# Weight gradient on one core: the second slice of X is loaded by the software DMA queue as bf16 instead of by a hardware queue as f32

## The chip, the cores and the metric

The kernel runs on one NeuronCore of one Trainium2 chip. The metric is the device time of one execution in microseconds (us). Profiles are of one execution each; they show the span from the first to the last instruction, which is somewhat shorter than the device time of the same execution.

Engines: TensorE (PE; PEld is its weight load), VectorE (DVE), ScalarE (ACT), GpSimd (POOL) and SyncE (SP). A DMA that SP or ACT issues runs on a hardware queue (q1 and q10 in this trace); one that POOL issues runs on the software queue (q0)[...].

## The reference

```
# input: [16, 512, 1024] f32, grad_output: [16, 512, 768] f32
grad_weight = np.einsum('bmk,bmn->kn', input, grad_output)   # [1024, 768] f32
```

With batch and m taken together this is X^T G with X of 8192 x 1024 and G of 8192 x 768: a sum over 8192 rows.

## The kernel before

**Slices and units.** The 8192 rows are cut into 64 slices of 128 rows (P = 128). A slice of X is 128 x 1024 and one of G 128 x 768. Two slices make a unit; there are 32 units, u = 0 to 31. A letter in LOADS (line 12) says how a unit is multiplied. For "s" (units 0 to 6, 30 and 31) each slice is multiplied on its own: X has a left and a right half of 512 columns, G of 384, and the four products of halves are the sums A (left, left), B (left, right), C (right, left) and D (right, right). For "P" (units 7 to 29) the two slices are treated as a 2 x 2 arrangement of blocks and multiplied with seven products (A, D, m, n, o, p, q) in place of eight; DVE first makes the sums and differences of blocks that these need (functions sum_g1 to sum_x3, lines 125 to 154).

**Matmuls.** Each product of halves takes four matmuls (q = 0 to 3, one for every 128 columns of the half of X) of 128 x 128 by 128 x 384 in bf16 (line 285), each into a PSUM bank of its own. Two slots of four banks are in use in turn. When a step closes, its banks are added to or copied into f32 sums in SBUF, by DVE (lines 301 and 303) or by ACT (line 299); before some steps ACT first puts the old sum into the bank (line 266).

**Order.** The engines' programs are written by hand. ORDER (lines 16 to 28) is a list of steps. "D1:1" means that product D is taken up to item 1 (an item is a slice of an "s" unit, or a "P" unit), and that ACT evicts one of its banks; "!" closes the step and evicts its banks. The first steps are A1, D1, C2, B2, D3, A2, B4, A3, C4, A4, D5, D6. A1 and D1 need slice 0 alone. C2 takes, for each q, first slice 0 and then slice 1, so its second matmul is the first to use slice 1. D3 begins the use of slice 2, B4 that of slice 3, D5 that of unit 2, B7 and B8 that of unit 3.

**Loads.** All of X and G comes from HBM as f32. From unit 2 on (u >= MERGED = 2), POOL issues one DMA for G and one for X of a whole unit (lines 106 and 107), which are rounded to bf16 on their way. Units 0 and 1 are loaded slice by slice, also by POOL (lines 111 and 113). Exceptions are G of slice 0 and X of slices 0 and 1. They are loaded as f32 into the tiles gf and xf[0], xf[1] by hardware queues: gf in two halves by SP (lines 81 and 83), xf[0] and xf[1] by ACT (lines 82 and 84). DVE and ACT then round them to bf16 (function round_by, line 206). X of slice 1 is rounded in four pieces ahead of step C2 (lines 361 to 366), the right half of gf ahead of D1 (line 360). POOL holds at most eight of its DMAs in flight: each issue waits until the eighth before it has landed. Tiles for X and G of unit 1 and later come from pools of 14 buffers each (PAIRS_HELD); xf[0], xf[1] and gf take their first buffers from the same pools.

**Start.** While the first operands are on their way, TensorE runs 12 warming matmuls on constants (lines 88 to 95).

Of the kernel before, what the change touches and what calls it, by code (L numbers as in the profile page):

```python
# [9 lines left out]
P = 128  # L10
# [28 lines left out]
MERGED = 2  # L39
# [3 lines left out]
def kernel(  # L43
# [6 lines left out]
    nc = tc.nc  # L50
    bf16 = mybir.dt.bfloat16
    f32 = mybir.dt.float32

    B, M, K = input.shape
# [6 lines left out]
    X = input.rearrange("b m k -> (b m) k")  # L61
# [4 lines left out]
    pairs = ctx.enter_context(tc.tile_pool(name="pairs", bufs=PAIRS_HELD))  # L66
# [9 lines left out]
    E = mybir.EngineType  # L76
    ctx.enter_context(tc.manual_schedule(engines={E.PE, E.DVE, E.Activation, E.Pool}))

    xf = [pairs.tile([P, K], f32, name=f"xf{s}", tag="xp") for s in range(2)]
    gf = pairs.tile([P, N], f32, name="gf", tag="gp")  # L80
    nc.sync.dma_start(out=gf[:, 0:NH], in_=G[0:P, 0:NH])  # L81
    nc.scalar.dma_start(out=xf[0], in_=X[0:P, :])
    nc.sync.dma_start(out=gf[:, NH:N], in_=G[0:P, NH:N])
    nc.scalar.dma_start(out=xf[1], in_=X[P : 2 * P, :])

    ones = nc.const_aps.tensor(1.0, (P, P), bf16)
    wps = psum.tile([P, 512], f32, name="bank7")
# [10 lines left out]
    items = []  # L98
    xg = []
    for u, kind in enumerate(LOADS):  # L100
        pool = pairs if u else head
        xp = pool.tile([P, 2, K], bf16, name="xp", tag="xp")
        gp = pool.tile([P, 2, N], bf16, name="gp", tag="gp")
        if u >= MERGED:
            rows = slice(2 * u * P, 2 * (u + 1) * P)
            nc.gpsimd.dma_start(out=gp, in_=G[rows, :].rearrange("(p m) n -> p m n", m=2))  # L106
            nc.gpsimd.dma_start(out=xp, in_=X[rows, :].rearrange("(p m) k -> p m k", m=2))  # L107
        for h in range(2):
            s = 2 * u + h
            if s > 0 and u < MERGED:  # L110
                nc.gpsimd.dma_start(out=gp[:, h, :], in_=G[s * P : (s + 1) * P, :])
            if s > 1 and u < MERGED:
                nc.gpsimd.dma_start(out=xp[:, h, :], in_=X[s * P : (s + 1) * P, :])
            if kind == "s":
                items.append(("s", xp[:, h, :], gp[:, h, :]))
        if kind == "P":
            items.append(("P", xp, gp))
        xg.append((xp, gp))
# [79 lines left out]
    def fill(n):  # L198
        for _ in range(n):
            f, i = filler.pop()  # L200
            f(i)


    def round_by(engine, dst, src, c0, c1):
        copy = nc.vector.tensor_copy if engine == "DVE" else nc.scalar.copy
        copy(out=dst[:, c0:c1], in_=src[:, c0:c1])  # L206

    x0, x1, g0 = items[0][1], items[1][1], items[0][2]
    round_by("DVE", g0, gf, 0, 192)
    round_by("ACT", g0, gf, 192, NH)  # L210
    round_by("DVE", x0, xf[0], 0, P)
# [35 lines left out]
    done = {p: 0 for p in streams}  # L247
# [101 lines left out]
            del opened[p]  # L349
            slots.append(slot)  # L350

    rounded = False
    for n, step in enumerate(ORDER):
        step, _, ahead = step.partition("!")
        step, _, byact = step.partition(":")
        byact, first = byact[:1], byact[1:]
        at = next(c for c in step if c.isalpha())
        before, upto = step.split(at)
        if n == 1:
            round_by("DVE", g0, gf, NH, N)  # L360
        if not rounded and done[at] < 2 <= int(upto):
            rounded = True
            round_by("DVE", x1, xf[1], 4 * P, 6 * P)
            round_by("ACT", x1, xf[1], 6 * P, 8 * P)
            round_by("DVE", x1, xf[1], 0, 2 * P)
            round_by("ACT", x1, xf[1], 2 * P, 4 * P)
        fill(int(before or 0))
        ahead = [int(a) for a in ahead.split(",")] if ahead else None
        visit(at, int(upto), int(byact or 0), first, ahead is not None, ahead, n == len(ORDER) - 1)
# [31 lines left out]
```

## Time and profile before

| | |
|---|---|
| device time, median of 3 runs | 163.57 us (163.35 to 163.69) |
| profiled execution | 163.7 us, span 161.9 us |
| PE busy | 157.1 us (97%), 951 matmuls |
| DVE busy | 139.6 us (86%) |
| ACT busy | 94.6 us (58%) |
| POOL busy | 34.6 us (21%) |
| HBM | 58.72 MB read, 3.15 MB written, 382 GB/s over the span |
| DMA by queue | software 28.64 MB (as written, bf16), hardware 3.47 and 1.11 MB |

The profile's groups of instructions give the operations around the change. xf is rounded by DVE in 222 to 295 ns a piece (128 or 256 columns) and by ACT in 401 to 405 ns (256 columns). The hardware DMAs of xf land 4.1 and 5.9 us after their issue, those of gf 3.8 and 5.5 us after it. POOL takes some 0.53 to 0.6 us for the issue of one DMA. The granted TensorE clock is full throughout.

How to read it: the busy share of an engine says little of what sets the time. The chain of work that ended last does: it is followed back from the last instruction, at each step to what released it. The page's sum of this chain is PE 93%, DMA 3%, DVE 1%. The timeline lists instructions in order of time, with the idle time before each in brackets and what ended it.

### The profile page before, as it was taken

The page shows a single profiled execution, that of the slowest core. Times are in us where ns is not written, and L with a number is a line of the kernel's source. Part 1 is how long each engine was busy: PE and PEld are TensorE (multiplying, and loading weights), DVE is VectorE, ACT ScalarE, POOL GpSimd, SP SyncE. Part 2 cuts the span into 40 slices and gives each one's busy share as a digit, 9 for nine tenths or more (in the row PEclk, how much of TensorE's full clock was granted, in tenths as well). Part 3 has the DMA queues.
Part 4 walks back from the last instruction along what each step waited for, and adds up shares of the span by engine and source line. Part 5 has one row for each costly group of instructions (what it writes and reads, how often), then busy time and mean ns, then how long its engine had stood idle before and what let it go on. Part 6 is the DMA issues. An engine that isn't in the chain of part 4 may idle for free.

```text
span 161.9 us, 2755 instructions
## 1 busy us (share of the span) xinstructions
PE 157.1 (97%) x951; PEld 92.7 (57%) x951; DVE 139.6 (86%) x289; ACT 94.6 (58%) x221; POOL 34.6 (21%) x69
## 2 busy tenths in 40 slices
PE   8799999999999999999999999999999999999992
PEld 2365666566565565655656666666555666666661
DVE  0557947469979999999989999999998999999992
ACT  3766004745587799359749684661446646888410
POOL 7442222122221212222212222222212100000000
PEclk9999999999999999999999999999999999999999
DMA  5999999999999999999999999999999999902675
GB/s 171 294 213 211 211 216 215 211 211 215 214 213 212 212 213 213 213 211 215 212 213 213 212 216 214 220 207 212 211 211 214 212 214 214 187 5 97 225 283 173
DMA packets 12397, 33.40 MB, mean 206 GB/s; under 512 B 1376, under 2 KB 4192, under 8 KB 12384
## 3 DMA queue, kind: packets, MB, share of 16 engines
q0 software_dynamic: 9360, 28.64, 89.4%
q1 hardware_dynamic: 2592, 3.47, 6.2%
q10 hardware_dynamic: 432, 1.11, 1.8%
q8 instruction: 7, 0.11, 0.3%
q14 instruction: 6, 0.05, 0.1%
HBM read 58.72 MB, written 3.15 MB: 382 GB/s over the span
## 4 chain that ended last, share of the span: by engine, by line
PE 93%; DMA 3%; DVE 1%; SPq 0%; issue 0%
PE bank L285 93%; DMA gf<-in_grad_output_dram 3%; PE bank L336 0%; DVE acc L344 0%; SPq L81 0%; DVE gp L206 0%
## 5 line engine op out<-in xcount | busy, mean ns | idle before, releaser
L285 PEld LDWEIGHTS <-xp 128*128 128x128 bf16 x649 | 63.3, 98 | 43.6 <-issue 1.5
L285 PE MATMUL bank<-gp,xp 128*128 128x384 bf16 x468 | 80.9, 326 | 1.0 <-DVE gp L206 1.0
L299 ACT COPY macc<-bank 128x384 f32<-128x384 f32 x73 | 31.5, 493 | 25.0 <-PE bank L285 24.9
L303 DVE TENSOR_TENSOR acc<-bank,acc 128x384 f32<-128x384 f32 x69 | 34.7, 551 | 8.7 <-PE bank L285 8.3
L285 PEld LDWEIGHTS <-xe 128*128 128x128 bf16 x276 | 26.6, 98 | 18.5 <-DVE xe L145 0.8
L285 PE MATMUL bank<-ge,xp 128*128 128x384 bf16 x181 | 33.6, 326 | 0.0
L285 PE MATMUL bank<-gp,xe 128*128 128x384 bf16 x184 | 32.4, 326 | 0.0
L266 ACT COPY bank<-macc 128x384 f32<-128x384 f32 x56 | 25.3, 503 | 8.0 <-DVE macc L303 6.9
L299 ACT COPY acc<-bank 128x384 f32<-128x384 f32 x44 | 19.5, 486 | 15.4 <-PE bank L285 15.3
L107 POOL DMA_DIRECT2D xp<-in_input_dram x30 | 15.9, 530 | 53.1 <-DMA xp<-in_input_dram 29.8
L106 POOL DMA_DIRECT2D gp<-in_grad_output_dram x30 | 15.9, 531 | 37.5 <-DMA gp<-in_grad_output_dram 14.8
L303 DVE TENSOR_TENSOR macc<-bank,macc 128x384 f32<-128x384 f32 x44 | 22.5, 552 | 1.5 <-PE bank L285 1.2
L266 ACT COPY bank<-acc 128x384 f32<-128x384 f32 x34 | 15.2, 492 | 8.6 <-DVE acc L303 8.5
L285 PE MATMUL bank<-ge,xe 128*128 128x384 bf16 x92 | 16.6, 326 | 0.0
L145 DVE TENSOR_TENSOR xe<-xp 128x1024 bf16<-128x1024 bf16 x23 | 15.7, 684 | 0.5 <-DMA xp<-in_input_dram 0.5
L154 DVE TENSOR_TENSOR xp<-xp 128x1024 bf16<-128x1024 bf16 x23 | 15.7, 684 | 0.0
L189 DVE TENSOR_TENSOR acc<-acc,macc 128x768 f32<-128x768 f32 (+1 forms) x20 | 14.6, 791 | 0.0
L131 DVE TENSOR_TENSOR ge<-gp 128x768 bf16<-128x768 bf16 x23 | 12.7, 551 | 0.2 <-DMA gp<-in_grad_output_dram 0.2
L140 DVE TENSOR_TENSOR gp<-gp 128x768 bf16<-128x768 bf16 x23 | 12.7, 551 | 0.0
L149 DVE TENSOR_TENSOR xe<-xp 128x512 bf16<-128x512 bf16 x23 | 9.6, 418 | 0.0
L135 DVE TENSOR_TENSOR ge<-gp 128x384 bf16<-128x384 bf16 x23 | 8.1, 351 | 0.0
L89 PE MATMUL bank<-const-bfloat16-1.0 128*128 128x512 bf16 (+1 forms) x12 | 4.6, 574 | 0.8 <-PEq L385 0.8
(20 smaller groups left out, 21.4 us busy)
## 6 DMA issues: line engine op xcount, KB each, us to landing
xp<-in_input_dram POOLq DMA_DIRECT2D x30, 512.0 KB, 16.7
gp<-in_grad_output_dram POOLq DMA_DIRECT2D x30, 384.0 KB, 16.7
out_dram<-acc SPq DMA_DIRECT2D x15, 192.0 KB, 1.9
xf<-in_input_dram ACTq DMA_DIRECT2D x2, 512.0 KB, 5.0
gp<-in_grad_output_dram POOLq DMA_DIRECT2D x3, 192.0 KB, 6.6
xp<-in_input_dram POOLq DMA_DIRECT2D x2, 256.0 KB, 7.9
gf<-in_grad_output_dram SPq DMA_DIRECT2D x2, 192.0 KB, 4.6
out_dram<-acc SPq DMA_DIRECT2D x1, 128.0 KB, 1.7
```

The costliest lines, as they stand in the source:

```text
L106: nc.gpsimd.dma_start(out=gp, in_=G[rows, :].rearrange("(p m) n -> p m n", m=2))
L107: nc.gpsimd.dma_start(out=xp, in_=X[rows, :].rearrange("(p m) k -> p m k", m=2))
L131: nc.vector.tensor_add(out=ge[:, 0:2, :], in0=g[:, :, 0, :], in1=g[:, :, 1, :])
L140: nc.vector.tensor_sub(out=g[:, 1:3, :], in0=g[:, 1:3, :], in1=g[:, 3::-3, :])
L145: nc.vector.tensor_add(out=xe[:, 0:2, :].rearrange("p a k -> p (a k)"), in0=xp[:, 0, :], in1=xp[:, 1, :])
L149: nc.vector.tensor_add(out=extra[i][0][:, 2, :], in0=xp[:, 0, 0:KH], in1=xp[:, 1, KH:K])
L154: nc.vector.tensor_sub(out=x[:, 1:3, :], in0=x[:, 1:3, :], in1=x[:, 0::3, :])
L189: op(out=dst, in0=dst, in1=src)
L266: nc.scalar.copy(out=bank, in_=sum_of(p, q))
L285: nc.tensor.matmul(bank, stat, mov, start=opening and j == 0 and not carried, stop=close and j == len(items_now) - 1, skip_group_check=car ...
L299: nc.scalar.copy(out=dst, in_=bank)
L303: nc.vector.tensor_add(out=dst, in0=bank, in1=dst)
```

## The change

X of slice 1 is no longer loaded as f32 by ACT's hardware queue and rounded by DVE and ACT. POOL loads it by the software queue, directly as bf16 into its tile, as the second of its DMAs: behind G of slice 1 and ahead of G of slice 2. The float tile xf[1] and the four casts are gone. Nothing else is edited; in particular ORDER is the same.

```diff
-    xf = [pairs.tile([P, K], f32, name=f"xf{s}", tag="xp") for s in range(2)]
+    xf = [pairs.tile([P, K], f32, name=f"xf{s}", tag="xp") for s in range(1)]
...
     nc.sync.dma_start(out=gf[:, NH:N], in_=G[0:P, NH:N])
-    nc.scalar.dma_start(out=xf[1], in_=X[P : 2 * P, :])
...
             if s > 0 and u < MERGED:
                 nc.gpsimd.dma_start(out=gp[:, h, :], in_=G[s * P : (s + 1) * P, :])
-            if s > 1 and u < MERGED:
+            if s > 0 and u < MERGED:
                 nc.gpsimd.dma_start(out=xp[:, h, :], in_=X[s * P : (s + 1) * P, :])
...
-    x0, x1, g0 = items[0][1], items[1][1], items[0][2]
+    x0, g0 = items[0][1], items[0][2]
...
-    rounded = False
...
-        if not rounded and done[at] < 2 <= int(upto):
-            rounded = True
-            round_by("DVE", x1, xf[1], 4 * P, 6 * P)
-            round_by("ACT", x1, xf[1], 6 * P, 8 * P)
-            round_by("DVE", x1, xf[1], 0, 2 * P)
-            round_by("ACT", x1, xf[1], 2 * P, 4 * P)
```

## The prediction

> **What bounds the kernel now.** I began with the page's chain of work that ended last, in order of time. Columns: start in us, length in us, what.
>
> ```profile
> 1.17 5.52 DMA gf<-in_grad_output_dram
> ...
> 6.71 0.37 DVE gp L206
> 7.08 0.04 issue
> 7.12 150.51 PE bank L285 x921
> 157.64 0.78 PE bank L336 x7
> ```
>
> From 7.12 us on the chain is TensorE alone. 921 matmuls in 150.51 us are 0.163 us each, so there is next to no idle time to win there. Before 7.12 stands a wait for the right half of G of slice 0 (gf), landed at 6.69, and its rounding. Any change of the start reaches the end only through this run of matmuls: by the time of its first ones, or by operands that come too late for one of them.
>
> So I asked next when transfers come. The DMA view cut at 5.3 us (queue, packets, MB written, share of 16 engines) has in its first part
>
> ```profile
> q10 hardware_dynamic: 209, 0.79, 38.4%
> q1 hardware_dynamic: 270, 0.38, 25.2%
> ```
>
> and, from 5.3 to 8 us, for the first time
>
> ```profile
> q0 software_dynamic: 295, 0.42, 86.2%
> ```
>
> **The software queue moves nothing before 5.33 us** (its first packet), though POOL issued its first DMA at 1.23. Until then only the hardware queues work, and xf[1] is 0.52 MB of what they move. The stretches (time, then busy time of each engine, clock, DMA share, GB/s written) give the rates:
>
> ```profile
> 4.50:5.30 0.80, 0.80 (x5) 0.42 (x4) 0.71 (x4) 0.78 (x3) 0.80 (x3) 1.00 0.99 374
> 6.50:16.00 9.50, 8.88 (x55) 5.31 (x55) 5.88 (x14) 6.64 (x17) 3.17 (x6) 1.00 1.12 212
> ```
>
> Software packets are written as bf16 and read as f32, so 212 GB/s written is 424 read. The engines are never idle between 3 and 16 us.
>
> Last, the slack of the operands. POOL's timeline shows when earlier transfers landed, since each issue waits for the eighth before it:
>
> ```profile
> 7.83 0.53 POOL L107 DMA_DIRECT2D xp<-in_input_dram  x1 [2.23 <-DMA gp<-in_grad_output_dram]
> 8.75 0.53 POOL L106 DMA_DIRECT2D gp<-in_grad_output_dram  x1 [0.39 <-DMA gp<-in_grad_output_dram]
> ...
> 16.52 0.53 POOL L107 DMA_DIRECT2D xp<-in_input_dram  x1 [1.93 <-DMA xp<-in_input_dram]
> ...
> 20.87 0.53 POOL L107 DMA_DIRECT2D xp<-in_input_dram  x1 [1.96 <-DMA xp<-in_input_dram]
> ```
>
> The last increment of the landing comes 0.29 us before: 7.54 (G of slice 1), 8.46 (G of slice 2), 16.24 (X of unit 2), 20.58 (X of unit 3). TensorE's first use, counted through the written order, is at 7.93, 10.53, 16.45 and 20.83. So X of unit 2 comes 0.21 us ahead of its use and X of unit 3 0.25. At 43.9 us there is none left:
>
> ```profile
> 43.91 0.69 DVE L145 TENSOR_TENSOR xe<-xp 128x1024 bf16<-128x1024 bf16 x1 [0.34 <-DMA xp<-in_input_dram]
> 43.93 0.93 PEld L285 LDWEIGHTS <-xp 128*128 128x128 bf16 x7 [0.28 <-DMA xp<-in_input_dram]
> ```
>
> X of unit 8 landed at 43.89 and TensorE loaded it 0.04 later, having waited. **TensorE follows the transfers closely**: a delay of the whole software queue comes through.
>
> **What the Trainium skill says.** "DMA: Bandwidth & Descriptors", section "Issuing engines are not separate DMA queues", says that all queues run on the same 16 engines, so a move between queues saves issue time alone. The trace agrees: 374 GB/s read by two hardware queues, 424 by the software queue alone, engines full in both. Its section "Latency and other measured facts" gives about 0.6 us to the first byte of a hardware DMA and about 1 us of a software one. The trace has 1.02 (0.74 to 1.76) and 4.10 (1.23 to 5.33); the measurement decides, and it is what this change turns on. Its section "SWDGE vs HWDGE vs iDMA" ties rounding in flight to the GpSimd queue, as this kernel does.
>
> **The change part by part.**
>
> Removed, at no gain: two DVE casts (0.50 us from 7.11) and two ACT casts (0.71 from 7.11) of xf[1]. DVE then idles 1.99 us before 9.60 and ACT 0.47 before 8.30, and TensorE runs through that time without a stop, so the casts are hidden. The ACT DMA issue (0.46 at 1.17) goes too; ACT waits for gf until 4.52 anyway.
>
> Added: one POOL issue, 0.55 us, in second place (the listing of the built program confirms it: G of slice 1, X of slice 1, G of slice 2). Later first issues move back by it: G of slice 2 from about 1.9 to 2.4, X of slice 2 from 2.41 to 2.96, all before 5.33, so nothing is lost on the queue. The wait for the eighth DMA before moves by one place; at least seven stay queued. X buffers: the float tile's slot goes, and X of unit u still takes over that of unit u-14. No cost.
>
> Moved earlier: the right half of gf. Without xf[1] the hardware queues have 0.39 + 0.52 = 0.92 MB; the packets reach that sum at 4.77 in the present trace, so it lands near 5.1 instead of 6.69. Its cast stands on DVE behind the first eviction (5.72 to 6.28), so it runs 6.28 to 6.64 and TensorE starts step D1 near 6.69 instead of 7.12: 0.43 us. But D1 is four matmuls (0.65) and step C2's first uses slice 0; its second needs X of slice 1, at 7.50.
>
> Moved later: X of slice 1. The software rate is (8.75 to 16.52: five transfers, 1600 KiB written, 7.77 us) 206 KiB/us. Engines start on that queue between 5.33 and about 5.7. G and X of slice 1 are 448 KiB, 2.18 us, so X lands at 7.5 to 7.9, and C2's second matmul starts at about 7.95; it is at 7.93 now. **The 0.43 us is waited away there**: nothing gained, nothing lost.
>
> Everything behind it: the queue carries 256 KiB more, 1.24 us. In return G of slice 1 no longer shares the engines with xf[1]: from last start to last landing it takes 7.54 - 5.70 = 1.84 now and would take 0.93 + 0.05; 0.86 back. Net 0.38; with the first start and landing (5.33, 7.08) it is 0.47. Other way round: the engines sit idle from 4.77 to about 5.5, 0.73; the 4480 KiB (read) up to X of unit 2 took 11.23 us from 4.77 and take 10.89 at the pure software rate, 0.34 back; 0.39. I take **+0.40 us for every later landing** (bounds: 1.24 with no relief; -0.34 with no idle).
>
> Then TensorE: X of unit 2 at 16.64, used at 16.69 instead of 16.45: +0.24. X of unit 3: 20.98, +0.05, against 20.83: +0.20, inside that. X of unit 8: no slack, +0.40. After it all other slacks are at least 0.42 (unit 15), so nothing is added, and the end moves by 0.40: the span 161.9 becomes 162.3. Run times stand 1.8 over the span (163.7 for the profiled one); on the median of 163.57 this gives 163.97, say 163.95.
>
> **The rivals.** A (forecast, 0.46): as above.
>
> B (0.20): unit 8's late landing is an accident of one execution. An instruction fetch of 16 KB sits on one DMA engine at 41.8 us, and landings round it spread over 2.2 us instead of 1.3 to 1.5. If that doesn't decide, unit 2's +0.24 does: 163.8. For it: a late single engine is fickle. Against: fetches are in the trace every 21 us and TensorE's course brings them to the same transfer.
>
> C, the other side (0.22): the 4.1 us to the first software packet are not fixed, but come from the full hardware queues. Emptied by 4.77, they let the software queue start at once; no engine idles, landings move by up to -0.34, D1's 0.43 is kept, and unit 8 bounds the gain: 163.2 to 163.5, in the middle 163.3. It decides if the first software packet comes before 4.93 (5.33 - 0.40). Against: it now starts on some 13 engines within 0.29 us while both hardware queues are still at work on most, which looks like a fixed delay rather than a queue that drained.
>
> D (0.12): less relief than I take, for instance half, 0.43: all landings +0.8, X of slice 1 after 8.3, 164.35.
>
> That the change doesn't do what it says is excluded by the listing.
>
> **How the numbers follow.** 0.2% (0.33 us, about what a measurement of this kernel can tell from no change) lies between A and B. Slower by more: four fifths of A (0.37), a little of B (0.03), D (0.12): 0.52. Faster by more: half of C, 0.11, taken as 0.12. The rest, 0.36, is within. The range leaves out C's better half and the outer half of D: 163.3 to 164.3.
>
> **What would show it.** Right: first software packet again near 5.33 and a gap in the DMA share from 4.8; the cast of gf's right half at 6.28; a second TensorE stop near 7.5 to 7.95; POOL's issues of 16.52 and 20.87 (now one place later in the queue) at 16.9 and 21.3; a TensorE wait for X of unit 2. Wrong: a software packet before 4.9, or landings of unit 2 no later than now; or a TensorE wait at 7.5 that lasts past 8.1.

## The result and the profile after

The changed kernel takes 164.41 us (median of 4 runs, 164.20 to 164.47) against 163.63 for the kernel before beside it (163.35 to 163.69): a ratio of 1.0048, 95% interval 1.0031 to 1.0066. It is 0.78 us slower (0.5 to 1.08), where +0.38 was forecast; 164.41 lies just above the range. The profiled spans are 162.58 and 161.94, so 0.64 us of it can be followed in the traces.

The chain of work that ended last, after the change, in order of time (start us, length us, what):

```profile
1.89 6.22 DMA xp<-in_input_dram
8.11 0.05 issue
8.16 8.69 PE bank L284 x52
16.84 0.01 issue
16.85 141.38 PE bank L284 x864
```

Before, the chain went over to TensorE at 7.12 and stayed there to the end. Now it runs through the software transfer of X of slice 1 (issued 1.89, landed 8.11) and through TensorE only from 8.16. It breaks a second time at 16.85, at X of unit 2, and then there are 864 matmuls in one piece. The kernel's loss must be made at these two places, or later inside that piece.

The timeline after (start us, busy us, engine, line, operation, count; in brackets the idle time before and what ended it):

```profile
6.25 0.35 DVE L205 CAST gp<-gf 128x384 bf16<-128x384 f32 x1
...
8.15 8.30 PEld L284 LDWEIGHTS <-xp 128*128 128x128 bf16 x52 [0.91 <-DMA xp<-in_input_dram]
16.85 4.18 PEld L284 LDWEIGHTS <-xp 128*128 128x128 bf16 x27 [0.39 <-DMA xp<-in_input_dram]
17.09 0.53 POOL L106 DMA_DIRECT2D xp<-in_input_dram  x1 [1.93 <-DMA xp<-in_input_dram]
21.44 0.53 POOL L106 DMA_DIRECT2D xp<-in_input_dram  x1 [1.97 <-DMA xp<-in_input_dram]
```

The cast of gf's right half runs at 6.25, 0.46 us earlier than before, as worked out. TensorE then waits for X of slice 1, and C2's second matmul starts at 8.16 (before 7.93). X of unit 2 landed at 16.80, 0.29 us ahead of the issue at 17.09; before it was 16.24. TensorE uses it at 16.85 instead of 16.45, **+0.40**. X of unit 3 landed at 21.15 (21.44 less 0.29), 0.09 ahead of its use, and adds nothing. At unit 8 TensorE has no wait any more: X landed at 43.36, 0.92 us before its use.

The DMA view after, for the stretch 4.3 to 5.3 us (queue, packets, MB written, share of 16 engines):

```profile
q0 software_dynamic: 81, 0.12, 73.4%
q1 hardware_dynamic: 94, 0.12, 32.6%
```

**The software queue no longer begins at 5.33 but at 4.34**, before the time (4.77) at which the prediction had the engines fall idle. Yet its first transfers were not the faster for it. In the stretches after (start:end, then length, busy time of each engine, clock, DMA share, GB/s written) this can be seen in the last column:

```profile
5.50:6.00 0.50, 0.50 (x3) 0.30 (x2) 0.23 (x1) 0.02 (x1) 0.09 (x1) 1.00 1.16 153
6.00:6.50 0.50, 0.50 (x3) 0.15 (x1) 0.50 (x2) 0.41 (x2) 0.00 (x0) 1.00 1.05 188
7.00:12.00 5.00, 4.47 (x28) 2.53 (x27) 1.89 (x4) 2.82 (x7) 2.28 (x5) 1.00 1.14 208
```

The DMA share is over 1 in all three, so no engine looks idle, and still only 153 GB/s are written at 5.50, against 208 later. The trace's records of single packets, which no view lists, say why. A software packet of G takes 135 ns as a rule, one of X 173. After the change seven packets that start at 5.62 to 6.10, among the first of X of slice 1, take over 200 ns more than that; the longest takes 842 ns, 669 too many. The kernel before has none in its trace (in a second execution two packets take 207 ns, 72 too many). The seven end at 6.08 to 6.72, and the landings of X of slice 1 then spread over about a microsecond (7.13 to 8.11).

Another 0.2 us come at the end of unit 8's work. ACT's first eviction of step A15, before and after:

```profile
43.48 0.97 ACT L299 COPY acc<-bank 128x384 f32<-128x384 f32 x2 [1.96 <-PE bank L285]
```

```profile
44.20 0.86 ACT L298 COPY acc<-bank 128x384 f32<-128x384 f32 x2 [2.27 <-PE bank L284]
```

It starts 0.72 later, where TensorE is only 0.35 late. Its releasing semaphore event is at 43.85, as it should be; the copy itself starts 0.35 us after that. ACT then paces the next step (0.22 us from one bank to the next instead of 0.16), and TensorE goes from +0.35 to +0.59 by 46.6 us.

### The profile page after: what moved, and what is told of

Same layout as the page of the kernel before. It is cut to its first block, busy times and chain, and to the rows that moved or that the text cites. A ratio compares the mean times of both kernels' runs of the same rounds, so it can differ in the third digit from the quotient of the medians.

```text
span 162.6 us, 2747 instructions
## 1 busy us (share of the span) xinstructions
PE 158.1 (97%) x951; PEld 92.6 (57%) x951; DVE 138.9 (85%) x287; ACT 93.7 (58%) x219; POOL 35.2 (22%) x70
## 4 chain that ended last, share of the span: by engine, by line
PE 93%; DMA 4%; issue 0%; DVE 0%; POOL 0%; POOLq 0%
PE bank L284 92%; DMA xp<-in_input_dram 4%; PE bank L335 0%; DVE acc L343 0%; POOL gp L110 0%; POOLq L377 0%
## 5 line engine op out<-in xcount | busy, mean ns | idle before, releaser
L300 DVE COPY acc<-bank 128x384 f32<-128x384 f32 x6 | 3.1, 553 | 3.9 <-PE bank L284 3.9
## 6 DMA issues: line engine op xcount, KB each, us to landing
gp<-in_grad_output_dram POOLq DMA_DIRECT2D x30, 384.0 KB, 16.9
```

## The experiments

A "padded" kernel holds one more ACT copy of one column ahead of the roundings; the reason comes with e7_pad. Ratios are against the kernel before, measured beside each, with 95% intervals. "Slow packets" are software packets that take over 200 ns more than the rule for their size; "too long" is what a packet takes over that rule.

**e1_swap: X ahead of G in the changed kernel.** It asks whether the order of the two transfers of slice 1 matters.

```diff
+            if s == 1:
+                nc.gpsimd.dma_start(out=xp[:, h, :], in_=X[s * P : (s + 1) * P, :])
             if s > 0 and u < MERGED:
                 nc.gpsimd.dma_start(out=gp[:, h, :], in_=G[s * P : (s + 1) * P, :])
-            if s > 0 and u < MERGED:
+            if s > 1 and u < MERGED:
                 nc.gpsimd.dma_start(out=xp[:, h, :], in_=X[s * P : (s + 1) * P, :])
```

> Changed kernel with the first two software DMAs swapped: X of slice 1 ahead of G of slice 1. Both are needed by the same matmul. In the changed kernel the first packets of X of slice 1 (2048 B written, normally 173 ns) take 400 to 840 ns on some seven DMA engines at 5.5 to 6.1 us, and last landings trail first ones by 0.8 us. If the stall belongs to this time or to the second place in the queue, it moves to G of slice 1 (packets of over 300 ns at 5.5 to 6.1) and the time stays at 164.4. If it belongs to X of slice 1 itself, its packets stall at 4.5 to 5 us instead. Either way last landings spread by 0.7 to 0.9 us and the time is 164.2 to 164.6. Rival (the spread is an accident of one execution): spread back to 0.45 and 164.0.

Measured: 164.00 us, ratio 1.0018 (0.9997 to 1.0038). Same bytes, same start (4.48), but no packet is slow (the longest takes 325 ns, 190 too many), and X of unit 2 lands at 16.39 instead of 16.80. TensorE reaches unit 2 at 16.43, no later than before; its loss of 0.17 in the profile all comes from the late ACT copy near 44 us. So most of the loss is not the bytes as such.

**e2_half: only the left half of X of slice 1 by the software queue** (from the kernel before).

```diff
-    nc.scalar.dma_start(out=xf[1], in_=X[P : 2 * P, :])
+    nc.scalar.dma_start(out=xf[1][:, KH:K], in_=X[P : 2 * P, KH:K])
...
+            if s == 1:
+                nc.gpsimd.dma_start(out=xp[:, h, 0:KH], in_=X[s * P : (s + 1) * P, 0:KH])
...
-            round_by("DVE", x1, xf[1], 0, 2 * P)
-            round_by("ACT", x1, xf[1], 2 * P, 4 * P)
```

> Half a dose, from the kernel before: the right half of X of slice 1 (256 KiB f32, what step C2 reads) stays on ACT's hardware queue and is rounded by the engines; the left half (step B2, needed 1.2 us later) comes by the software queue. Theory (the software queue starts on an engine when SP's queue has drained there, and the extra 256 KiB are made up for by the earlier start, so what costs is X of slice 1 landing last at 8.1): no wait at C2 beyond 7.93, software start near 4.8, X of unit 2 last at about 16.4; 163.6 to 163.9. Rival (cost is proportional to what is moved to the software queue): half of +0.78, 164.0.

Measured: 164.14, ratio 1.0054 (1.0018 to 1.0091), slower than expected. Four of the eleven executions took 165.4 to 165.8, which pulls the ratio up; the median alone is 1.0027 of the one beside it. C2's second matmul came at 7.59, 0.34 earlier than before, but X of unit 2 landed at 16.88 and TensorE lost 0.45. The software queue began only at 5.34: on each engine its first packet follows the end of xf[1]'s remaining half there, not that of gf. So here it started no earlier than before and had 128 KiB more to move. A faster start of C2 thus wins nothing: what comes through is the landing of unit 2.

**e3_sp: the float X of slice 1 on SP's queue**, behind gf, instead of ACT's (from the kernel before). It asks whether the software queue waits until SP's queue has drained.

```diff
-    nc.scalar.dma_start(out=xf[1], in_=X[P : 2 * P, :])
+    nc.sync.dma_start(out=xf[1], in_=X[P : 2 * P, :])
```

> Kernel before with xf[1] issued by SP behind the right half of gf, instead of by ACT. Theory (the software queue waits on each engine until SP's queue has drained): the first software packet comes only near 6.3, at the end of xf[1], though ACT's queue is empty from 4.5; G of slice 1 lands last at 7.6 to 8.0. The right half of gf lands near 5.1 and D1 starts at about 6.7. Rival (the software queue starts when its share of engine time is free, whichever queue holds it): first packet near 4.5 to 5. Time by the theory 163.4 to 164.0: later landings unchanged within 0.2 us, since the bytes are the same.

Measured: 164.30, ratio 1.0040 (1.0024 to 1.0056). The software queue began at 4.49, though SP's queue had xf[1] to move up to 7.9. The theory of the drained queue fell. What did end at 4.49 is the right half of gf. The loss, which had not been expected, is made at C2: xf[1], last on SP's queue, landed at 8.25, and C2's second matmul started at 8.62 instead of 7.93. Nothing is added at unit 2.

**e4_gr_act: that right half on ACT's queue** (from the changed kernel).

```diff
-    nc.sync.dma_start(out=gf[:, NH:N], in_=G[0:P, NH:N])
+    nc.scalar.dma_start(out=gf[:, NH:N], in_=G[0:P, NH:N])
```

> Changed kernel with the right half of gf issued by ACT behind xf[0], so that SP's queue holds only the left half of gf. Theory (software queue waits for SP's queue): SP's queue drains near 3.7, first software packet at 3.7 to 4.1, sharing with ACT's queue until about 5; landings of the software queue move by at most -0.3, since the same bytes come at the same rate. Rival (it waits for all hardware queues, or for a time of about 4.3): first packet at 4.3 or later. Time 164.2 to 164.5 in both.

Measured: 164.23, ratio 1.0030 (1.0005 to 1.0054). The first software packet is at 4.56, and gf's right half ends at 4.57 on ACT's queue. So in e3, e4 and the changed kernel, on two queues, the first software packet comes when gf's right half is through on an engine. In the kernel before, the first one comes 0.16 us after gf's right half first ends (5.17), with xf[1] still under way. There are 12 slow packets before 8 us, the longest of 911 ns.

**e5_act_rounds: all rounding of slice 0 by ACT.** It asks whether DVE's casts hold up the software transfers. The Trainium skill, "SBUF — State Buffer", section "SBUF: two separate sides", says that some DVE copies keep GpSimd from writing the descriptors of such transfers.

```diff
-    round_by("DVE", g0, gf, 0, 192)
...
-    round_by("ACT", x0, xf[0], 6 * P, 8 * P)
+    round_by("ACT", g0, gf, 0, NH)
+    round_by("ACT", x0, xf[0], 0, 4 * P)
+    round_by("ACT", x0, xf[0], 4 * P, 8 * P)
+    round_by("ACT", g0, gf, NH, N)
...
-        if n == 1:
-            round_by("DVE", g0, gf, NH, N)
```

> Changed kernel with all rounding of slice 0 on ACT and none on DVE. Question: why do the first packets of X of slice 1 take 250 to 840 ns in place of 173 on about eight DMA engines near 5.5 to 6.1 us. Theory L (DVE's casts from SBUF to SBUF, 4.8 to 5.4 and from 6.25 us, hold up the writing of descriptors by GpSimd): without them no such packets, last landing of X of slice 1 within 0.5 us of the first and near 7.7. Theory O (it is the order G then X at the start of the queue, since the swapped order had few): the slow packets stay, last landing 8.0 to 8.3. The time itself tells little, since ACT rounds for longer: 164.0 to 164.6.

Measured: 164.18, ratio 1.0037 (1.0022 to 1.0051). The slow packets are still there (8, the longest of 794 ns) and X of unit 2 lands at 16.78. So DVE's casts don't make them; this case gives no sign of that lock.

**e7_pad: the changed kernel with one more ACT copy.** The late copy near 44 us is number 65 of ACT's program in the changed kernel and in e1, each with 307 instructions; in kernels with 308 to 310 it isn't late. The edit moves it by one place.

```diff
+    spare = accp.tile([P, 1], f32, name="spare")
+    nc.scalar.copy(out=spare, in_=ones[:, 0:1])
```

> Changed kernel with one ACT instruction more at the start, a copy of one column into a spare tile. In the changed kernel ACT's first eviction of step A15, at 44.2 us, starts 0.35 us after its semaphore is there, and the next 0.24; ACT then paces step m2, whose four banks each cost TensorE 0.06 us: +0.18 to +0.24. The swapped kernel has the same, the kernels with one or more ACT instructions more have not. Theory (the place of the instruction in ACT's program, 307 instructions against 308 to 310, where it is the 65th): no such lag, TensorE's delay stays at +0.40 to +0.45 against before, time 164.15 to 164.25. Rival (chance or the moment, not the place): lag as in the changed kernel, 164.35 to 164.5.

Measured: 164.36, ratio 1.0047 (1.0035 to 1.0059). The late copy is gone, TensorE stands at +0.62 before it and +0.59 after it, but the time is no better: in this execution X of slice 1 landed at 8.32 and X of unit 2 at 17.02. So the lag is a matter of an instruction's place, and in times it can't be told from the scatter of the landings. The later variants are padded, except e10, which has 308 instructions by its own edit.

**e8_swap_pad: X ahead of G, padded.**

> X of slice 1 ahead of G of slice 1, and one ACT instruction more. If the order and the place of ACT's instruction are the two causes, both are away here: no lag at step A15, TensorE at that step within 0.1 us of before, time 163.6 to 163.85, the same as before. If the lag stays: 164.0 as without the instruction.

Measured: 163.86, ratio 1.0018 (1.0000 to 1.0036). The end of its chain of waits:

```profile
16.48 0.05 issue
16.52 141.17 PE bank L288 x864
```

Unit 2 is reached at 16.52 (changed kernel 16.85, kernel before 16.45), and the 864 matmuls take 141.17 instead of 141.38. In this profile next to nothing is left of either loss: the span is 162.1, against 161.9. The ratio, though, is that of e1, which had the lag. The two are the best of all variants, and still not faster than the kernel before.

**e9_gr_sw: gf's right half by the software queue as well**, first of all its transfers (from e8).

```diff
-    nc.sync.dma_start(out=gf[:, NH:N], in_=G[0:P, NH:N])
...
+            if s == 0:
+                nc.gpsimd.dma_start(out=gp[:, 0, NH:N], in_=G[0:P, NH:N])
...
-        if n == 1:
-            round_by("DVE", g0, gf, NH, N)
```

> As the last, and the right half of G of slice 0 also comes by the software queue, first in it (no cast by DVE). In six runs so far the software queue's first packet on each engine starts at the end of that engine's share of this very transfer, on whichever hardware queue. Theory (it waits for the hardware transfers issued before it): the hardware queues now end near 4.0 to 4.4 and the first software packet comes at 3.9 to 4.1, landings of X of unit 2 by up to 0.3 us earlier than before (last at 15.9 to 16.2); time 163.4 to 163.7. Rival (the software queue cannot start before about 4.3 us): first packet at 4.3 to 4.5, engines idle for some 0.3 us, X of unit 2 last at 16.2 to 16.5; time 163.7 to 163.9.

Measured: 165.37, ratio 1.0122 (1.0095 to 1.0148). The start came earlier, at 4.09 on the first engine, and D1 at 5.84. On every engine the first software packet now comes within about 6 ns of the end of xf[0], the last hardware transfer left there (4.08 to 4.51). So it isn't gf's right half as such that holds the queue back. But two packets took 1233 and 1568 ns, G of slice 1 landed over 7.16 to 8.90, and TensorE got C2's second matmul at 8.94, a microsecond later than before, and the expected 163.4 to 163.7 was missed. The queue began earlier, and its slow packets grew longer.

**e10_both: the changed kernel, with the hardware transfer of xf[1] put back**, into a tile that nobody reads. The 256 KiB are then moved twice.

```diff
-    xf = [... for s in range(1)]
+    xf = [... for s in range(2)]
...
+    nc.scalar.dma_start(out=xf[1], in_=X[P : 2 * P, :])
```

> Changed kernel, but ACT's hardware queue also loads X of slice 1 as f32 into xf[1], which nothing reads; the output is complete. Question: is it the software queue having the engines to itself at its start that makes X of slice 1 slow? Theory (yes): as in the kernel before, the software queue starts at about 5.3 beside xf[1] and none of its packets before 8 us takes more than 60 ns over the normal; last landings within 0.5 us of the first; all software landings 1.1 to 1.25 us later than before (256 KiB more at 206 KiB/us), X of unit 2 last at 17.3 to 17.5, TensorE +1.0 to +1.1, time 164.6 to 164.8. Rival (it is X of slice 1 by this queue, whatever runs beside it): slow packets of 250 to 900 ns again, spread 0.8 or more, X of unit 2 last at 17.7 or later, time 165 or more.

Measured: 164.78, ratio 1.0077 (1.0062 to 1.0092). The end of its chain of waits, and its stretch at 5.5 us:

```profile
8.98 8.69 PE bank L285 x52
...
17.70 141.18 PE bank L285 x864
```

```profile
5.50:6.00 0.50, 0.50 (x4) 0.28 (x3) 0.32 (x1) 0.27 (x2) 0.10 (x1) 1.00 1.03 309
```

No slow packet at all; the queue starts at 5.29, and 309 GB/s are written at 5.50, part of them by the hardware queue, which writes f32. The unread transfer fills the time. X of unit 2 lands 1.21 (first) to 1.41 us (last) later than in the kernel before, and TensorE uses it 1.25 later: **this is what 256 KiB more on the software queue cost with no relief**, computed as 1.24.

**e11_rows: other addresses.** Slices 1 and 3 change places in memory, X and G alike; the sum is the same.

```diff
+            r = (0, 3, 2, 1)[s] * P
...
-                nc.gpsimd.dma_start(out=gp[:, h, :], in_=G[s * P : (s + 1) * P, :])
+                nc.gpsimd.dma_start(out=gp[:, h, :], in_=G[r : r + P, :])
```

> Changed kernel with the ACT instruction of the padded one, and with the rows of slices 1 and 3 exchanged (the sum over slices is the same): the same transfers in the same places, from other addresses. Theory A (address: the rows of slice 1 next to those of slice 0 just read): the slow packets at 5.5 to 6.1 go away, X of slice 1 lands within 0.5 us and the time is 163.8 to 164.0. Theory O (the place behind a G at the start of the queue): they stay, last landing of this transfer at 8.0 to 8.3, time 164.2 to 164.4.

Measured: 164.23, ratio 1.0040 (1.0025 to 1.0055); four slow packets that end at the same times (6.07 to 6.60 us), the longest of 832 ns. It isn't the address.

**e12_split: X of slice 1 in two transfers**, with packets of half the size.

```diff
-            if s > 0 and u < MERGED:
+            if s == 1:
+                nc.gpsimd.dma_start(out=xp[:, h, KH:K], in_=X[s * P : (s + 1) * P, KH:K])
+                nc.gpsimd.dma_start(out=xp[:, h, 0:KH], in_=X[s * P : (s + 1) * P, 0:KH])
+            if s > 1 and u < MERGED:
```

> Padded changed kernel with X of slice 1 in two software DMAs, the right half first, which is all that step C2 reads; packets of 1024 bytes written in place of 2048. If what delays TensorE at 8.1 is the wait for the whole of X of slice 1, C2's second matmul comes at 7.2 to 7.6 in place of 8.16, and the rest of the delay is decided by unit 2. Theory (the stall belongs to the second transfer of the queue): the right half's packets are slow again, X of unit 2 last at 16.6 to 17.0, time 164.1 to 164.4. Rival (long packets alone stall): no packets over 60 ns too long, X of unit 2 last at 16.2 to 16.5, time 163.7 to 164.0.

Measured: 164.82, ratio 1.0095 (1.006 to 1.013). Seven slow packets before 7 us, the longest of 1195 ns, the last ending at 6.98. C2's second matmul came at 8.12, not at the hoped-for 7.2 to 7.6. The stretch at 6 us shows the gap plainly, in the DMA share too:

```profile
6.00:6.50 0.50, 0.07 (x1) 0.07 (x1) 0.38 (x2) 0.50 (x3) 0.00 (x0) 1.00 0.57 91
```

It isn't the size of the packets either. The variant also has one more issue ahead of the later ones; whether that makes it the slower one isn't shown.

**before_again: the kernel before, profiled once more.**

> The kernel before, unchanged, for a second profile. The prediction took from one execution that X of unit 8 lands last at 43.89 and that TensorE waits for it. If that recurs in place: a TensorE wait of about 0.2 us at 43.7 to 44 again. If it was an accident: unit 8 lands last by 43.2 and the wait is not there; steps after 46 us then come at most 0.2 us earlier or are paced by ACT's evictions.

Measured: 163.68, ratio 1.0002 (0.9983 to 1.0021). Its timeline at unit 8:

```profile
43.89 0.60 PEld L285 LDWEIGHTS <-xp 128*128 128x128 bf16 x5 [0.40 <-DMA xp<-in_input_dram]
```

X of unit 8 comes late again, at 43.85; the weight load sits idle for 0.40 us, of which the matmuls lose some 0.18. So this was no accident of one execution, as rival B had it, but it belongs to the kernel before: in the changed kernel, e1, e3, e4, e5, e7, e8 and e11 the landing is at 43.0 to 43.5. (In e2, built from the kernel before, it is at 44.31.) The wait also swallows gains: up to there TensorE was 0.16 us ahead of the first execution, after it only 0.04.

In both executions of the kernel before, the instruction fetch that rival B names takes one DMA engine for 0.94 us from 41.8, just when unit 8 lands, and the landings of unit 8 spread over 2.2 us instead of 1.3 to 1.4. In the changed kernel the fetch comes at 42.41, and the spread is 1.51, as for the units ahead of it. But in e2 it comes nearly as late, at 42.27, and the spread is 2.48. That the fetch is the cause is thus possible, not shown.

**e13_hold: POOL busy with memsets between X of slice 1 and G of slice 2** (padded). The next issues are held back, so that nothing they do can disturb X of slice 1.

```diff
                 nc.gpsimd.dma_start(out=xp[:, h, :], in_=X[s * P : (s + 1) * P, :])
+                if s == 1:
+                    hold = accp.tile([P, 256], f32, name="hold")
+                    for _ in range(6):
+                        nc.gpsimd.memset(hold, 0.0)
```

> Padded changed kernel; after it has issued G and X of slice 1, GpSimd fills a spare tile six times before it issues the next transfer. Theory (issues of later transfers delay the descriptors of the second): no packets of X of slice 1 over 373 ns, last landing 7.4 to 7.7, X of unit 2 last at 16.2 to 16.5, time 163.6 to 164.0. Rival (a fixed readiness, or the queue's own start): slow packets as before with ends at 6.0 to 7.0, X of slice 1 last at 7.9 to 8.3, time 164.1 to 164.5.

Measured: 164.59, ratio 1.0063 (1.0044 to 1.0082). X of slice 1 now lands over 7.11 to 7.74, its longest packet takes 465 ns (292 too many), and C2's second matmul is at 7.79, 0.37 earlier than in the changed kernel. But X of slice 2, issued at 5.06, has packets of 0.95 to 1.21 us at 7.85 to 8.19, which end at 8.86 to 9.41. The stretch shows them as the same dent at a later time:

```profile
8.00:8.50 0.50, 0.50 (x5) 0.31 (x4) 0.00 (x0) 0.34 (x1) 0.50 (x2) 1.00 0.91 133
```

The dent has moved with the issues. X of unit 2 landed at 17.31 and not at the expected 16.2 to 16.5, so the hold helped one transfer and cost more at the next.

**e14_late: POOL's first issue held back** from 1.23 to 2.10 us by four memsets (padded). If the start of the software queue is a fixed time after the issue, it moves by 0.87.

> Padded changed kernel; GpSimd fills a spare tile four times before its first issue, so that every issue comes later by the time that this takes (d, 1 to 2 us), and the hardware queues end as before at 4.9. If readiness follows the issue: the first software packet at 4.1 + d or later, ends of the slow packets later by d too, the landing of X of slice 1 later by about d. If the slow packets come from the moment at which the hardware queues run empty: their ends stay at 6 to 7. Time 164.5 + 0.7 d or so in the first case.

Measured: 165.35, ratio 1.0113 (1.0057 to 1.0169). The first packet came at 4.35, as without the hold: 2.25 us after the issue instead of 3.1. It isn't a fixed time after the issue. X of slice 1, however, landed over 7.05 to 9.15, slow packets ended as late as 8.57, and C2's second matmul came at 9.20, a microsecond later. In this profile late issues thus cost at the tail of the transfers what they don't cost at their start. The time says less: the four executions took 164.61, 164.65, 166.04 and 166.58, and the profile is of the last, which lost 1.6 us more to a drop of TensorE's clock (see the end).

## Why the prediction was wrong

**The direction and the path were right.** The casts of xf[1] gave nothing. gf's right half was cast at 6.25 (said: 6.28). The gain in D1 was waited away at C2. The loss came through X of unit 2, for which TensorE waits, and the two POOL issues moved to 17.09 and 21.44 (said: 16.9 and 21.3).

**The first step that failed is "the software queue moves nothing before 5.33 us", taken as fixed.** It started at 4.34, ahead of the 4.93 named as the point from which rival C decides. On every DMA engine the first software packet follows the end of gf's right half, which had been slowed by xf[1]. The records don't name a packet's engine, but the times pair off: in the changed kernel each of the 16 ends has a first software packet within 40 ns, 13 of them within 5 to 7 ns. The other variants built from the changed kernel, e9 and e10 aside, show the same, and so does e3. In e9, without that transfer, the packets follow xf[0], and in e2 the rest of xf[1]. So what holds the queue back on an engine is hardware transfers already queued there. A fixed delay is contradicted by e14, a wait for a whole queue to drain by e3. Why xf[1] in its full size does not hold it back in the kernel before, in e3 and in e10, no run shows. The Trainium skill, "DMA: Bandwidth & Descriptors", section "SWDGE vs HWDGE vs iDMA", has each engine serve its queues in turn; that holds here for the full xf[1] (both queues at work together in e3), not for the transfers named before.

**Rival C nevertheless gave no gain,** and this is the second failure, in the term "0.86 back". Between the bare cost of 1.24 (e10: 1.21 to 1.41) and the changed kernel (first landing of X of unit 2 +0.17, mean +0.30, last +0.56) the relief came: in the mean 0.94, somewhat more than assumed. On the last engine it was 1.24 - 0.56 = 0.68, and TensorE waits for the last engine. The relief was computed as a volume on sixteen equal engines, and it came unequally: on single packets 0.2 to 0.7 us were lost.

The slow packets account for the mean as well. Add up what all software packets before 16.2 us take too long, and divide by 16 engines: 0.28 us in the changed kernel, against the mean of +0.30; in e1 0.05 against +0.08, in e7 0.30 against +0.30. In the seven kernels with these same transfers (the changed kernel, e1, e4, e5, e7, e8, e11) the two agree within 0.11 us. By this estimate the bytes as such would have cost nearly nothing: the earlier start gave back almost all of the 1.24, and what remained is the slow packets. The gain of up to 0.34 that rival C saw without idle engines is in none of these runs either; e1, with hardly a packet too long, still lands X of unit 2 0.05 to 0.15 later than before.

Across e4, e5, e7 and e11, which leave the transfers of the changed kernel as they are but for gf's queue or the addresses, the last landing of X of unit 2 is +0.47 to +0.78, never 0.40. The prediction's unit 2 use was 16.69; it came at 16.85. By its time the result is nearest to rival D (164.35), but D's picture, half the relief and all landings +0.8, isn't what the trace shows.

What the slow packets are is argued, not shown. The reading that fits the most runs: a software transfer has its packets ready on the slowest engine only 3.8 to 5 us after POOL issues it (changed kernel: issued 1.89, last slow packet ends 6.72, 4.8 later; e13: issued 5.06, ends up to 9.41, 4.35 later; e12: about 5), and an engine that reaches it earlier sits in one of its first packets until then. In the kernel before, xf[1]'s hardware transfer lasts until 6.7 and fills just that time. For it: the stall vanishes when that transfer is put back (e10), moves with the issues (e13), grows with an earlier start (e9), and doesn't depend on DVE, address or packet size (e5, e11, e12). Against a fixed readiness time: X ahead of G (e1, e8) has only milder stalls, at most 190 and 390 ns too long, and e2 has some packets 105 to 276 ns too long though its queue starts at 5.34. A second reading stands beside it, that POOL's later issues hold up the packets of earlier ones: holding them back nearly freed X of slice 1 in e13. No run tells the two apart. Under the first reading **removing xf[1] from the hardware queues freed time that the software queue was not yet able to use**; part of what came back was lost again in slow packets.

**The unit 8 step failed as well.** "X of unit 8: no slack, +0.40" carried the forecast from +0.24 to +0.40. The late landing is a property of the kernel before (before_again), but the shifted kernel doesn't have it: X of unit 8 lands at 43.36 and TensorE goes through at +0.35. That TensorE stands near the forecast +0.40 there is luck: the forecast was put together from a unit 2 term too small by 0.16 and a unit 8 term that is not there.

**On top came a term that no step had**, ACT's late start at 44.20. In the profile it takes TensorE from +0.35 to +0.59; e7 and e8 are without it. In the times its removal can't be seen (e7 against the changed kernel, e8 against e1), so it is shown for the profiled execution and open for the median.

The sum then reads: +0.40 at unit 2, -0.05 up to unit 8, +0.24 at ACT, +0.05 at the tail: 0.64 in the span, against 0.78 (0.5 to 1.08) in the times. Whether the rest is more than scatter isn't settled. No version beat the kernel before: X ahead of G undoes about two thirds of the loss (1.0018 against 1.0048, with intervals that just overlap); its packets are hardly slowed, and X of unit 2 lands last at +0.15 instead of +0.56.

## What to carry to other kernels

Before counting on the time that a transfer frees on the DMA engines, ask whether the other queue can use it. Here putting the hardware transfer back, though nobody read it, took away every slow packet (e10); it had looked like a competitor and had filled time that the software queue used badly. And ask what the first packet of a queue waits for: here its delay followed the hardware transfers ahead of it, and was no constant. Compute a landing for the slowest engine, not from volume and a mean rate, and read GB/s beside the DMA share: the share was over 1 while a quarter of the rate was missing. A zero slack in one execution is not a term to add by itself, since a shifted kernel may not have it; look first whether the operand comes late for a reason that shifts along.

## What was unexpected in the hardware

**The start of the software queue.** Its first packet came 2.25 us (e14) to 4.1 us (the kernel before) after the issue. The Trainium skill, "DMA: Bandwidth & Descriptors", section "Latency and other measured facts", gives about 1 us; none of these runs shows it. Since the first packet follows a hardware transfer in nearly all of them, they don't show the queue's own latency either; 2.25 us is an upper bound for e14.

**ACT's late copy.** In the two programs with 307 ACT instructions, number 65 started late, in the changed kernel 0.35 us after its semaphore event; with one instruction more ahead of it, it did not. What happens at that place in the program is open.

**TensorE's clock in e14.** After 1.51 us without a matmul TensorE was granted about half its clock in the profiled execution (the stretches; the clock is the third column from the end):

```profile
8.00:9.20 1.20, 0.00 (x1) 0.01 (x1) 0.00 (x0) 0.00 (x0) 0.54 (x1) 0.95 1.13 202
9.20:12.60 3.40, 3.40 (x12) 1.65 (x13) 0.30 (x1) 1.92 (x4) 1.64 (x4) 0.52 1.12 209
12.60:20.00 7.40, 7.40 (x47) 4.42 (x46) 5.88 (x13) 4.06 (x9) 2.09 (x5) 1.00 1.07 213
```

In 9.20 to 12.60 us the clock is 0.52 and a matmul takes 0.32 us instead of 0.16; some ten of them cost 1.6 us. In e9's profile TensorE had a longer pause, 2.12 us, and kept its full clock, so the length of the wait alone doesn't decide.
